# A short-sequence attention kernel: the whole output held on chip and stored in one run, four buffers for q and k, and an empty first trip of TensorE's loop

## The chip, the cores and the metric

The kernel runs on one core of a Trainium2 chip. A core has five engines that run their own instruction streams and meet only at semaphores: TensorE (PE; its weight loads are listed apart as PEld), VectorE (DVE), ScalarE (ACT), GpSimd (POOL) and SyncE (SP). Data move between the chip's main memory (HBM) and the on-chip memory (SBUF) by 16 DMA engines. Here GpSimd issues all loads and SyncE all stores. TensorE writes to PSUM, from which VectorE and ScalarE carry results to SBUF.

The metric is the device time of one execution in microseconds (us). The profile is one execution of its own, taken by the hardware profiler; its span runs from the first to the last instruction.

## The reference

For 32 x 12 heads, each with 128 rows of 64 elements, the kernel computes softmax attention:

```python
# q, k, v: (32, 12, 128, 64) float32
scale = 1.0 / np.sqrt(q.shape[-1])
scores = scale * np.matmul(q, k.transpose(0, 1, 3, 2))
attn = np.exp(scores - scores_max)
attn = attn / (np.sum(attn, axis=-1, keepdims=True) + 1e-8)
return np.matmul(attn, v).astype(np.float32)
```

Each of q, k, v and the output is 12.58 MB in float32. The loads cast to bf16 on the way, so 37.75 MB are read and 18.87 MB written into SBUF; the output is stored in float32.

## The kernel before

The work is cut into 48 units of 8 heads. Four units make a group (a "super" in the code). A group needs one load of q, one of k and one of v, 512 KB each as written in bf16, so there are 12 of each. The output goes out in 48 transfers of 256 KB.

A load brings many rows of a head into one partition, so that the runs in memory are long. TensorE then puts things in order: it transposes pairs of rows of q and k (through `pair`), and reorders v by matmuls with a selection matrix. A unit is then: scores (q times k), exp on ScalarE, values (times v, with a column of ones that gives the sum), and on VectorE the reciprocal and the product (`normalise`).

```python
NQ, NVB, NVE, NP, NT, NA, NO = 8, 2, 8, 4, 2, 4, 10      # buffers: q and k, v, ..., output
LATE, LOADED = 14, NU - 12                               # NU = 48

q_b = [sb(f"q_b{i}", [128, 2, 16 * D], bf16) for i in range(NQ)]
v_b = [sb(f"v_b{i}", [128, 4, RV * D], bf16) for i in range(NVB)]
o_sb = [sb(f"o_sb{i}", [128, 2 * 2 * RO * D], f32) for i in range(NO)]
# ... cut
```

The program is written in steps. In step u each engine gets, in this order: TensorE the transposes of a group ahead (T), the ordering of v of unit u+3 (V), the scores of u+1 (S) and the values of u (O); ScalarE copies the ordered v (K) and takes the exps of u+1; VectorE normalises u-1 (N), carries the transposes from PSUM (E) and makes the pairs for step u+2 (P), which is where it waits for loads.

```python
for u in steps:
    for t in t_at.get(u, []):        pe_transposes(t)
    for m in v_at.get(u, []):        pe_order_v(m); act_keep(m)      # m = u + 3
    if 0 <= u + 1 < NU:              pe_scores(u + 1); act_exps(u + 1)
    if 0 <= u < NU:                  pe_values(u)
    if 0 <= u - 1:                   dve_normalise(u - 1)
    for t in t_at.get(u, []):        dve_keep(t)
    for t in t_at.get(u + 2, []):    dve_pair(t)                     # waits for q or k, and for v
    # ... cut
```

GpSimd issues the loads in the order in which they are first needed: q0 k0 v0 q1 k1 v1 q2 k2 v2 q3 k3 v3 and so on. Each has a wait for its buffer:

```python
if kind == "v":
    if x >= NVB:                     # until v of the group two before is ordered
        deps = [("V", sum(vgroups[:x - NVB + 1]) - 1)]
    # ... cut
if x >= NQ:                          # q, k: until the pairs of the group NQ before are made
    deps = [("P", t) for t in t_order if t[0] == x - NQ and t[1] == j]
```

SyncE issues the stores. A store waits for its last unit plus `LATE` units, but not beyond unit 36, and the output buffers are used in turn, so `normalise` waits for the store ten before:

```python
last = first + n - 1
op("SP", ("store", c), emit, [("N", max(last, min(last + LATE, LOADED)))])

def dve_normalise(u):
    c, w, n, first = splace[u]
    dma = []
    if w == 0 and c >= NO:
        dma.append((s_o[c % NO], sum(16 * pieces(x) for x in range(c % NO, c, NO))))
    # ... cut
```

VectorE tells SyncE and GpSimd of its progress by marks on the pair copies (and, near the end, on `normalise` itself), so a store leaves after the first such mark behind the unit that it waits for.

TensorE's program is a loop of 7 trips, 8 steps to a trip. What does not exist in the first or in the last trip is skipped by a branch; a wait counts its semaphore down, so the same instructions serve each trip:

```python
nc.tensor.reg_mov(trip, 0)
with nc.tensor.Fori(0, TRIPS):
    for skipped, always, some in places:
        run_waits("PE", always)
        with nc.tensor.If_ne(trip, skipped):
            for o, w in some:
                run("PE", o, w)
    nc.tensor.reg_add(trip, trip, 1)
```

Of the kernel before, what the change touches and what calls it, by code (L numbers as in the profile page):

```python
# [10 lines left out]
def kernel(  # L11
# [7 lines left out]
    nc = tc.nc  # L19
    f32 = mybir.dt.float32  # L20
# [3 lines left out]
    B, H, S, D = q.shape  # L24
# [7 lines left out]
    NU = B * H // 8  # L32
    RO, SO = 4, S // 4
# [25 lines left out]
    stores = [1, 1] + [2] * ((NU - 4) // 2) + [1, 1]  # L59
# [5 lines left out]

    PERIOD = 8
    TRIPS = NU // PERIOD + 1


    t_at, v_at = {}, {}
    for s, (R, f) in enumerate(supers):
        J = R // 4
        for x in range(J):
            j, b = divmod(x, J // 2)
# [2 lines left out]
        v_at[m - 3] = [m]  # L79
    steps = range(min(t_at) - 2, NU + 1)  # L80

    NQ, NVB, NVE, NP, NT, NA, NO = 8, 2, 8, 4, 2, 4, 10

    LATE, LOADED = 14, NU - 12

    def sb(name, shape, dtype):
        return ctx.enter_context(nc.sbuf_tensor(name, shape, dtype))
# [11 lines left out]
    pair = [sb(f"pair{i}", [128, 8, 2, D], bf16) for i in range(NP)]  # L99
    qkT = [sb(f"qkT{i}", [128, 2, 16, S], bf16) for i in range(NT)]  # L100
    attnT = [sb(f"attnT{i}", [128, 2, 4, S], bf16) for i in range(NA)]
    o_sb = [sb(f"o_sb{i}", [128, 2 * 2 * RO * D], f32) for i in range(NO)]
    recip = [sb(f"recip{i}", [128, 2, RO], f32) for i in range(2)]
    qk_ps = ps("qk_ps", [128, 8 * S], bf16)
    s_ps = [ps(f"s_ps{i}", [128, 2, 4 * S], f32) for i in range(2)]
# [9 lines left out]
    sems = {name: tc.alloc_semaphore(name) for name in MARKS}  # L115
# [7 lines left out]
    def op(engine, key, emit, deps=(), marks=(), dma=()):  # L123
        o = Op()
        o.key, o.emit, o.deps, o.marks, o.dma = key, emit, deps, marks, dma
        assert key not in position, key
        position[key], engine_of[key] = len(program[engine]), engine
        program[engine].append(o)

    def counts():  # L130
        c = {}
        for name, e in MARKS.items():
            n, at = 0, []
            for o in program[e]:
                n += name in o.marks
                at.append(n)
            c[name] = at
        return c
# [120 lines left out]
    def normalise(u):  # L259
        c, w, n, first = splace[u]  # L260
        o4 = o_ps[:, :, :RO * (D + 1)].rearrange("p a (r e) -> p a r e", e=D + 1)
        r = recip[u % 2]
        nc.vector.reciprocal(r[:], o4[:, :, :, D]).then_inc(s_r, 1)  # L263
        nc.vector.wait_ge(s_r, u + 1)
        o = o_sb[c % NO][:, :n * 2 * RO * D].rearrange("p (a w e) -> p a w e", a=2, w=n)
        return nc.vector.tensor_mul(  # L266
            o[:, :, w, :].rearrange("p a (r d) -> p a r d", d=D),
            o4[:, :, :, :D],
            r[:].unsqueeze(3).to_broadcast([128, 2, RO, D]))
# [6 lines left out]
    s_q = [tc.alloc_semaphore(f"s_q{i}") for i in range(NQ)]  # L276
    s_k = [tc.alloc_semaphore(f"s_k{i}") for i in range(NQ)]
    s_v = [tc.alloc_semaphore(f"s_v{i}") for i in range(NVB)]
    s_o = [tc.alloc_semaphore(f"s_o{i}") for i in range(NO)]
    v_readers = {}  # L280
    for u in range(NU):
        for a in range(2):
# [58 lines left out]

    def dve_normalise(u):
        c, w, n, first = splace[u]
        dma = []
        if w == 0 and c >= NO:
            dma.append((s_o[c % NO], sum(16 * pieces(x) for x in range(c % NO, c, NO))))

        marks = ["dve_pe"] + (["dve_io"] if u + 8 > t_step[t_order[-1]] else [])
        op("DVE", ("N", u), lambda: normalise(u), [("O", u)], marks, dma)

    def pieces(c):

        first = sum(stores[:c])
        return 2 if 1 < stores[c] < supers[of_unit[first]][0] // 4 else 1

    def sp_store(c):
        n = stores[c]
        first = sum(stores[:c])
        R, f = supers[of_unit[first]]
        J = R // 4  # L360

        def emit():
            dst = o_rows[:, 2 * f:2 * f + 2 * J, :].rearrange("p (a w) e -> p a w e", a=2)[
                :, :, first - f:first - f + n, :]
            src = o_sb[c % NO][:, :n * 2 * RO * D].rearrange("p (a w e) -> p a w e", a=2, w=n)
            if pieces(c) == 1:
                nc.sync.dma_start(out=dst, in_=src).then_inc(s_o[c % NO], 16)
            else:
                for a in range(2):
                    nc.sync.dma_start(out=dst[:, a], in_=src[:, a]).then_inc(s_o[c % NO], 16)  # L370

        last = first + n - 1
        op("SP", ("store", c), emit, [("N", max(last, min(last + LATE, LOADED)))])

    def pool_load(kind, x):
        deps = []
# [50 lines left out]
    for c in range(len(stores)):  # L427
        sp_store(c)
# [10 lines left out]
    for _, kind, x in loads:  # L439
        pool_load(kind, x)  # L440

    c = counts()
# [4 lines left out]
    def waits_of(engine, o):  # L447
        out = []
        for name, value in needed(engine, o, c).items():
            have = seen[engine].get(name, 0)  # L450
            if value > have:
                out.append((name, value - have if engine == "PE" else value))
                seen[engine][name] = value
        return out

    def run_waits(engine, waits):
        for name, value in waits:
            i = ENGINE[engine].wait_ge(sems[name], value)  # L458
            if engine == "PE":
                i.then_inc(sems[name], -value)  # L460

    def run(engine, o, waits):
# [5 lines left out]
        for n, name in enumerate(o.marks):  # L468
            (i if n == 0 else e.drain()).then_inc(sems[name], 1)

    def tensor_program():

        ops, waits, when = {}, {}, {}
        for o in program["PE"]:
            place = at_step[o.key] % PERIOD, o.key[0]
            w = waits_of("PE", o)
            assert waits.setdefault(place, w) == w and not o.dma, (o.key, w, waits[place])
            when.setdefault(place, []).append((at_step[o.key] // PERIOD + 1, o.emit is None))
            if at_step[o.key] // PERIOD == 2:
                ops[place] = o  # L480
        places = []
        for place in [(l, kind) for l in range(PERIOD) for kind in "TVSO"]:
            trips = [t for t, empty in when[place] if not empty]
            assert trips in (list(range(TRIPS - 1)), list(range(1, TRIPS))), (place, trips)
            waiting = len(when[place]) > len(trips)
            assert not waiting or len(when[place]) == TRIPS
            skipped = 0 if trips[0] else TRIPS - 1
            if waiting or not places or places[-1][0] != skipped:
                places.append((skipped, waits[place] if waiting else [], []))
            places[-1][2].append((ops[place], [] if waiting else waits[place]))  # L490
        trip = ctx.enter_context(nc.tensor.register("trip"))
        nc.tensor.reg_mov(trip, 0)
        with nc.tensor.Fori(0, TRIPS):
            for skipped, always, some in places:
                run_waits("PE", always)
                with nc.tensor.If_ne(trip, skipped):
                    for o, w in some:
                        run("PE", o, w)
            nc.tensor.reg_add(trip, trip, 1)

    with nc.Block() as block:
        @block.gpsimd
        def _(_e):
            for i, o in enumerate(program["POOL"]):
                if i == 2:
                    nc.gpsimd.wait_ge(s_zero, 1)
                    nc.gpsimd.affine_select(  # L507
                        out=ident[:], in_=ident[:], compare_op=mybir.AluOpType.not_equal,
                        fill=1.0, base=0, pattern=[[-1, 128]], channel_multiplier=1,
                    ).then_inc(s_id, 1)  # L510
                run("POOL", o, waits_of("POOL", o))

        @block.tensor
        def _(_e):
            tensor_program()

        @block.scalar
        def _(_e):
            for o in program["ACT"]:
                run("ACT", o, waits_of("ACT", o))  # L520

        @block.vector
        def _(_e):
            for t in sel.values():
                nc.vector.memset(t[:], 0.0)  # L525
            nc.vector.memset(ident[:], 0.0).then_inc(s_zero, 1)
            for t in v_e:
                nc.vector.memset(t[:, :, D:D + 1], 1.0)
            nc.vector.wait_ge(s_id, 1)

            for jv in range(2):
                nc.vector.tensor_copy(  # L532
                    sel[16][:].rearrange("p h v (x y s) -> p h v x y s", x=2, y=2)[:, :, jv, :, jv, :],
                    ident[:].rearrange("p (h s x) -> p h x s", h=8, x=2))
            for o in program["DVE"]:
                run("DVE", o, waits_of("DVE", o))

        @block.sync
        def _(_e):
            for o in program["SP"]:  # L540
                run("SP", o, waits_of("SP", o))
            for i in range(NO):
                nc.sync.wait_ge(s_o[i], sum(16 * pieces(x) for x in range(i, len(stores), NO)))


# [28 lines left out]
```

The softmax here doesn't subtract the row's maximum and nothing guards it: scores larger than these inputs give would overflow.

## Time and profile before

| | before |
|---|---|
| time, median of 3 runs (us) | 142.29 (142.08 to 142.77) |
| span of the profiled execution (us) | 141.3 |
| busy: PE, DVE, ACT, POOL (us) | 97.5, 89.8, 74.2, 26.8 |
| mean granted TensorE clock | 0.923 |
| read from HBM, written to it (MB) | 37.75, 12.58 |
| issues of the stores, first to last (us) | 57.1 to 136.9 |
| issues of v's loads, first to last (us) | 3.3 to 110.7 |

How to read the profile: the page cuts the span into 40 slices, and each digit is a busy share in tenths; under it stand the GB/s that the DMA engines moved (as written). A window line gives, for a stretch A:B, its length, the busy time and count of instructions of each engine, the granted clock, the share of the 16 DMA engines that was busy (it can exceed 1, as packets overlap), and GB/s. A wait line reads: who waited, at which line of the kernel, for whom, then the total in us, how often, and the longest. A timeline line reads: start, length, engine, line, operation, tiles, count, and in brackets the idle time before it and what ended it; "issue" is time in which the engine waited for nothing that the profile shows. The records hold each DMA packet as well, with its queue, size and time.

### The profile page before, as it was taken

To read this page: it belongs to the slowest core of one execution; us is meant where nothing else is said; L and a number is where in the kernel's file an instruction comes from. 1 tells how busy PE (TensorE), PEld (TensorE's weight loads), DVE (VectorE), ACT (ScalarE), POOL (GpSimd) and SP (SyncE) were. 2 spreads that over 40 slices of the span, in tenths; PEclk is the share of its full clock that TensorE was granted. 3 is DMA by queue.
4 is the path that set the end of the run, shared out by engine and by line. 5 is a ranking of instruction groups with operands and counts; after the bars stand their busy time and mean duration, and the time that the engine had idled before them with its cause. 6 is when DMAs were issued, how large, how long until landed. Compare 5 with 4: busy or idle time off the path is not lost. (4 is left out here: it accounts for less than half of the span.)

```text
span 141.3 us, 6998 instructions
## 1 busy us (share of the span) xinstructions
PE 97.5 (69%) x3072; PEld 68.9 (49%) x3072; DVE 89.8 (64%) x204; ACT 74.2 (52%) x97; POOL 26.8 (19%) x41
## 2 busy tenths in 40 slices
PE   0051939999959789796695698595594798597510
PEld 0041625766646566574463465373363466465310
DVE  2143632989779696974963964964974767685540
ACT  3000206877847758576375177284484447559800
POOL 6910000506060240601402401400600200000000
PEclk9999996999999999999999689999999559999855
DMA  2999999699999999999999999999999999999982
GB/s 14 186 206 211 202 206 179 81 210 188 181 200 143 212 189 187 219 176 235 246 236 240 253 236 240 252 235 242 253 235 241 255 206 313 379 382 369 335 281 77
DMA packets 25928, 31.55 MB, mean 223 GB/s; under 512 B 1345, under 2 KB 19777, under 8 KB 25921
## 3 DMA queue, kind: packets, MB, share of 16 engines
q0 software_dynamic: 12864, 18.88, 76.5%
q1 hardware_dynamic: 13056, 12.59, 28.0%
q8 instruction: 4, 0.07, 0.2%
q14 instruction: 4, 0.02, 0.0%
HBM read 37.75 MB, written 12.58 MB: 356 GB/s over the span
## 5 line engine op out<-in xcount | busy, mean ns | idle before, releaser
L231 ACT CAST v_e<-v_ps 128x512 bf16<-128x512 f32 x48 | 28.2, 588 | 58.4 <-PE v_ps L185 58.4
L236 ACT ACTIVATE attnT<-s_ps 128x1024 bf16<-128x1024 f32 x48 | 49.4, 1029 | 0.3 <-PE s_ps L211 0.2
L171 PE MATMUL qk_ps<-ident,pair 128*128 128x128 bf16 x384 | 32.5, 233 | 16.5 <-PEq L458 15.7
L254 DVE COPY qkT<-qk_ps 128x1024 bf16<-128x1024 bf16 x48 | 32.8, 683 | 6.1 <-PE qk_ps L171 5.0
L185 PE MATMUL v_ps<-v_b,sel 128*32 128x256 bf16 x768 | 33.0, 295 | 3.1 <-issue 2.1
L171 PEld LDWEIGHTS qk_ps<-ident,pair 128*128 128x128 bf16 x384 | 24.3, 104 | 21.5 <-issue 20.6
L266 DVE TENSOR_TENSOR o_sb<-o_ps,recip 128x512 f32<-128x512 f32 x48 | 33.2, 691 | 1.7
L223 PE MATMUL o_ps<-v_e,attnT 128*32 128x65 bf16 x1536 | 21.7, 200 | 18.2 <-PEq L458 18.1
L223 PEld LDWEIGHTS o_ps<-v_e,attnT 128*32 128x32 bf16 x1536 | 16.1, 100 | 24.2 <-issue 21.2
L381 POOL DMA_DIRECT2D v_b<-in_v_dram x12 | 9.2, 770 | 83.4 <-PE v_ps L185 83.4
L245 DVE COPY pair<-k_b 128x1024 bf16<-128x1024 bf16 x24 | 11.0, 460 | 20.2 <-DMA v_b<-in_v_dram 20.2
L185 PEld LDWEIGHTS v_ps<-v_b,sel 128*32 128x32 bf16 x768 | 17.2, 100 | 9.6 <-issue 4.5
L211 PE MATMUL s_ps<-qkT 64*128 64x128 bf16 x384 | 19.9, 226 | 0.6 <-PEq L458 0.5
L263 DVE RECIPROCAL recip<-o_ps 128x8 f32<-128x8 f32 x48 | 9.7, 202 | 12.9 <-PE o_ps L223 6.6
L211 PEld LDWEIGHTS s_ps<-qkT 64*128 64x128 bf16 x384 | 11.3, 97 | 11.5 <-issue 11.5
L245 DVE COPY pair<-q_b 128x1024 bf16<-128x1024 bf16 x24 | 10.1, 422 | 3.4 <-DMA q_b<-in_q_dram 3.2
L393 POOL DMA_DIRECT2D q_b<-in_q_dram x12 | 8.7, 727 | 1.0 <-SPq L92 1.0
L393 POOL DMA_DIRECT2D k_b<-in_k_dram x12 | 8.8, 734 | 0.0
L231 ACT ACT_TABLE_LOAD x1 | 1.3, 1283 | 1.0 <-SPq L92 1.0
L532 DVE COPY sel<-ident 128x128 bf16<-128x128 bf16 x2 | 0.4, 225 | 1.7 <-POOL ident L507 1.7
L525 DVE MEMSET sel<- 128x256 uint32 x1 | 0.3, 272 | 1.1 <-SPq L92 1.1
L507 POOL TENSOR_SCALAR_AFFINE_SELECT ident<-ident 128x128 bf16<-128x128 bf16 x1 | 0.3, 312 | 0.1
(6 smaller groups left out, 0.8 us busy)
## 6 DMA issues: line engine op xcount, KB each, us to landing
out_dram<-o_sb SPq DMA_DIRECT2D x48, 256.0 KB, 7.0
q_b<-in_q_dram POOLq DMA_DIRECT2D x12, 512.0 KB, 11.4
k_b<-in_k_dram POOLq DMA_DIRECT2D x12, 512.0 KB, 13.5
v_b<-in_v_dram POOLq DMA_DIRECT2D x12, 512.0 KB, 9.8
```

The lines of the kernel that those rows point to most:

```text
L171: i = nc.tensor.transpose(p[:, :, r4, jj, :], x[:, r].rearrange("p a d -> p (a d)"), ident[:])
L185: x = nc.tensor.matmul(t[r4 * 32:(r4 + 1) * 32, i, :, :], lhsT=pick[:, w * nh + i, jv, :], rhs=v_b[g % NVB][:, :n, (4 * jv + r4) * D:(4 * ...
L211: i = nc.tensor.matmul(t[:, a, h, :], lhsT=x[p, 1, 4 * w + h, :], rhs=x[p, 0, 4 * w + h, :], start=True, stop=True)
L223: y = nc.tensor.matmul(t[h * SO:(h + 1) * SO, a, r * (D + 1):(r + 1) * (D + 1)], lhsT=x[:, a, h, r * SO:(r + 1) * SO], rhs=v_e[m % NVE][:, ...
L231: return nc.scalar.copy(v_e[m % NVE][:, :, :D], v_ps[:].rearrange("p (n e) -> p n e", e=D))
L236: return nc.scalar.activation(out=attnT[u % NA][:].rearrange("p a h (r s j) -> p (a h r) s j", r=4, j=J), in_=s_ps[u % 2][:].rearrange("p ...
L245: return nc.vector.tensor_copy(pair[t_index[t] % NP][:], src[:, 8 * b:8 * b + 8])
L254: return nc.vector.tensor_copy(x.rearrange("p h (r j s) -> p (h r) j s", r=4, j=J)[:, :, 2 * b:2 * b + 2, :].rearrange("p x j s -> p x (j ...
L263: nc.vector.reciprocal(r[:], o4[:, :, :, D]).then_inc(s_r, 1)
L266: return nc.vector.tensor_mul(o[:, :, w, :].rearrange("p a (r d) -> p a r d", d=D), o4[:, :, :, :D], r[:].unsqueeze(3).to_broadcast([128, ...
L381: op("POOL", ("load", kind, x), lambda: nc.gpsimd.dma_start(out=v_b[x % NVB][:, :n, :], in_=v_rows[:, first:first + n, :],).then_inc(s_v[x ...
L393: nc.gpsimd.dma_start(out=bufs[x % NQ][:], in_=rows[R][:, n:n + 2, :]).then_inc(sm[x % NQ], 16)
```

## The change

Three things change. First, each output transfer has a buffer of its own (96 KB for each partition in all), `normalise` no longer waits for stores, and no store is issued before unit 34 is normalised; the stores then follow one another as units are done. The aim is to part the loads from the stores. Second, q and k get four buffers each instead of eight, which frees the room. Third, TensorE's loop gets one more trip, ahead of the others, in which every block is skipped; ScalarE and VectorE raise the semaphores by what the waits of that trip count down. It is meant to bring the loop's instructions onto the chip while the first loads are under way.

```diff
-    NQ, NVB, NVE, NP, NT, NA, NO = 8, 2, 8, 4, 2, 4, 10
-    LATE, LOADED = 14, NU - 12
+    NQ, NVB, NVE, NP, NT, NA = 4, 2, 8, 4, 2, 4
+    HELD = NU - 14
-    o_sb = [sb(f"o_sb{i}", [128, 2 * 2 * RO * D], f32) for i in range(NO)]
+    o_sb = [sb(f"o_sb{c}", [128, n * 2 * RO * D], f32) for c, n in enumerate(stores)]
@@ dve_normalise
-        dma = []
-        if w == 0 and c >= NO:
-            dma.append((s_o[c % NO], sum(16 * pieces(x) for x in range(c % NO, c, NO))))
@@ sp_store
-        op("SP", ("store", c), emit, [("N", max(last, min(last + LATE, LOADED)))])
+        op("SP", ("store", c), emit, [("N", max(last, HELD))])
@@ tensor_program
+        for skipped, always, some in places:
+            for name, value in always:
+                extra[name] = extra.get(name, 0) + value
-        nc.tensor.reg_mov(trip, 0)
-        with nc.tensor.Fori(0, TRIPS):
+        for r, x in ((trip, 0), (step, 2), (a, 0), (b, 0)):
+            nc.tensor.reg_mov(r, x)
+        with nc.tensor.Fori(0, TRIPS + 1):
             for skipped, always, some in places:
                 run_waits("PE", always)
-                with nc.tensor.If_ne(trip, skipped):
+                with nc.tensor.If_ne(b if skipped else a, 0):
                     for o, w in some:
                         run("PE", o, w)
-            nc.tensor.reg_add(trip, trip, 1)
+            nc.tensor.reg_add(trip, trip, step)
+            nc.tensor.reg_mov(step, 1)
+            nc.tensor.reg_add(a, trip, 1)
+            nc.tensor.reg_alu(a, a, 2, mybir.AluOpType.logical_shift_right)
+            nc.tensor.reg_alu(b, trip, 7, mybir.AluOpType.bitwise_and)
@@ scalar and vector, ahead of their programs
+            nc.scalar.drain().then_inc(sems["act_pe"], extra["act_pe"])
+            nc.vector.drain().then_inc(sems["dve_pe"], extra["dve_pe"])
@@ cut: the stores' semaphores, ten before, are four now
```

More of the change, by code (lines that the diff above doesn't have):

```diff
@@ L264, in normalise @@
         nc.vector.wait_ge(s_r, u + 1)
-        o = o_sb[c % NO][:, :n * 2 * RO * D].rearrange("p (a w e) -> p a w e", a=2, w=n)
+        o = o_sb[c][:].rearrange("p (a w e) -> p a w e", a=2, w=n)
         return nc.vector.tensor_mul(
@@ L278 @@
     s_v = [tc.alloc_semaphore(f"s_v{i}") for i in range(NVB)]
-    s_o = [tc.alloc_semaphore(f"s_o{i}") for i in range(NO)]
+    s_o = [tc.alloc_semaphore(f"s_o{i}") for i in range(4)]
     v_readers = {}
@@ L343, in dve_normalise @@
         c, w, n, first = splace[u]
-        dma = []
-        if w == 0 and c >= NO:
-            dma.append((s_o[c % NO], sum(16 * pieces(x) for x in range(c % NO, c, NO))))
         marks = ["dve_pe"] + (["dve_io"] if u + 8 > t_step[t_order[-1]] else [])
-        op("DVE", ("N", u), lambda: normalise(u), [("O", u)], marks, dma)
+        op("DVE", ("N", u), lambda: normalise(u), [("O", u)], marks)
     def pieces(c):
@@ L364, in emit @@
                 :, :, first - f:first - f + n, :]
-            src = o_sb[c % NO][:, :n * 2 * RO * D].rearrange("p (a w e) -> p a w e", a=2, w=n)
+            src = o_sb[c][:].rearrange("p (a w e) -> p a w e", a=2, w=n)
             if pieces(c) == 1:
-                nc.sync.dma_start(out=dst, in_=src).then_inc(s_o[c % NO], 16)
+                nc.sync.dma_start(out=dst, in_=src).then_inc(s_o[c % 4], 16)
             else:
                 for a in range(2):
-                    nc.sync.dma_start(out=dst[:, a], in_=src[:, a]).then_inc(s_o[c % NO], 16)
+                    nc.sync.dma_start(out=dst[:, a], in_=src[:, a]).then_inc(s_o[c % 4], 16)
         last = first + n - 1
-        op("SP", ("store", c), emit, [("N", max(last, min(last + LATE, LOADED)))])
+        op("SP", ("store", c), emit, [("N", max(last, HELD))])
     def pool_load(kind, x):
@@ L469, in run @@
             (i if n == 0 else e.drain()).then_inc(sems[name], 1)
+    extra = {}
     def tensor_program():
@@ L490, in tensor_program @@
             places[-1][2].append((ops[place], [] if waiting else waits[place]))
-        trip = ctx.enter_context(nc.tensor.register("trip"))
-        nc.tensor.reg_mov(trip, 0)
-        with nc.tensor.Fori(0, TRIPS):
+        for skipped, always, some in places:
+            for name, value in always:
+                extra[name] = extra.get(name, 0) + value
+        trip, step, a, b = (ctx.enter_context(nc.tensor.register(x)) for x in ("trip", "step", "a", "b"))
+        assert TRIPS == 7
+        for r, x in ((trip, 0), (step, 2), (a, 0), (b, 0)):
+            nc.tensor.reg_mov(r, x)
+        with nc.tensor.Fori(0, TRIPS + 1):
             for skipped, always, some in places:
                 run_waits("PE", always)
-                with nc.tensor.If_ne(trip, skipped):
+                with nc.tensor.If_ne(b if skipped else a, 0):
                     for o, w in some:
                         run("PE", o, w)
-            nc.tensor.reg_add(trip, trip, 1)
+            nc.tensor.reg_add(trip, trip, step)
[3 more added lines that the diff above has]
+            nc.tensor.reg_alu(b, trip, 7, mybir.AluOpType.bitwise_and)
     with nc.Block() as block:
@@ L541, in _ @@
                 run("SP", o, waits_of("SP", o))
-            for i in range(NO):
-                nc.sync.wait_ge(s_o[i], sum(16 * pieces(x) for x in range(i, len(stores), NO)))
+            for i in range(4):
+                nc.sync.wait_ge(s_o[i], sum(16 * pieces(x) for x in range(i, len(stores), 4)))
 _INS = ['q', 'k', 'v']
```

## The prediction

> **What bounds the kernel now.** I first read the slices of the page and the DMA queues, then the windows cut where the traffic changes, then the waits, and last the order of work in the first 30 us. The chain that ended last is of little use: it goes back only 1.7 us, from the last unit's output to its matmuls.
>
> The page's slices (40 of 3.53 us) and its queue list:
>
> ```profile
> DMA  2999999699999999999999999999999999999982
> GB/s 14 186 206 211 202 206 179 81 210 188 181 200 143 212 189 187 219 176 235 246 236 240 253 236 240 252 235 242 253 235 241 255 206 313 379 382 369 335 281 77
> q0 software_dynamic: 12864, 18.88, 76.5%
> q1 hardware_dynamic: 13056, 12.59, 28.0%
> q8 instruction: 4, 0.07, 0.2%
> ```
>
> The DMA engines are busy almost throughout, while PE is busy for 69% and DVE for 64% of the span. The bound is the traffic: 18.88 MB of loads (counted as written, in bf16; twice that is read) on q0 and 12.59 MB of stores on q1. The windows give the rates (last columns: granted clock, DMA share, GB/s):
>
> ```profile
> 3.00:6.00 3.00, 0.00 (x0) 0.00 (x0) 0.36 (x2) 0.00 (x0) 2.92 (x6) 1.00 1.02 156
> 6.00:24.00 18.00, 10.18 (x120) 6.65 (x120) 7.01 (x14) 2.73 (x4) 1.67 (x3) 0.91 1.15 207
> 24.00:27.00 3.00, 3.00 (x116) 2.31 (x112) 2.26 (x7) 2.58 (x4) 2.15 (x3) 1.00 0.35 39
> 27.00:42.00 15.00, 12.77 (x449) 9.20 (x447) 12.58 (x28) 11.03 (x15) 4.36 (x6) 1.00 1.12 194
> 42.00:45.00 3.00, 3.00 (x107) 2.10 (x108) 2.94 (x6) 1.83 (x3) 0.02 (x1) 1.00 0.86 133
> 45.00:57.00 12.00, 10.52 (x376) 7.62 (x371) 9.40 (x23) 8.75 (x12) 2.15 (x3) 1.00 1.13 194
> 66.00:111.00 45.00, 32.21 (x1040) 22.58 (x1032) 30.06 (x67) 24.76 (x34) 9.09 (x13) 0.94 1.14 242
> 117.00:129.00 12.00, 9.34 (x356) 6.75 (x352) 8.69 (x18) 8.03 (x11) 0.00 (x0) 1.00 1.10 364
> 129.00:138.00 9.00, 4.04 (x192) 2.78 (x176) 4.50 (x10) 4.57 (x6) 0.00 (x0) 0.73 0.93 317
> 138.00:141.30 3.30, 0.00 (x0) 0.00 (x0) 0.00 (x0) 0.00 (x0) 0.00 (x0) 0.50 0.20 67
> ```
>
> Loads alone run at 194 to 207 GB/s, stores alone at 380 (the slices 379 and 382), both together at 242. Two holes stand out while there are loads left to do: 24 to 27 us (39 GB/s) and 42 to 45 us (133). The waits, the timeline of TensorE and that of GpSimd say where the first comes from:
>
> ```profile
> POOL v_b L381 <- PE v_ps L185: 83.4, 10, 16.7
> DVE recip L263 <- DMA out_dram<-o_sb: 6.3, 6, 2.1
> ```
>
> ```profile
> 18.15 0.27 PE L185 MATMUL v_ps<-v_b,sel 128*32 128x256 bf16 x1 [0.22 <-PEq L458]
> 20.57 1.04 PE L185 MATMUL v_ps<-v_b,sel 128*32 128x256 bf16 x15 [2.15 <-issue]
> ```
>
> ```profile
> 24.41 0.74 POOL L381 DMA_DIRECT2D v_b<-in_v_dram  x1 [16.75 <-PE v_ps L185]
> ```
>
> GpSimd issues all loads in one order; v has two buffers, so group 2 of v (and all of q and k behind it) waits until TensorE has ordered v of unit 3. That came at 24.1 us, because TensorE stood still for 2.15 us inside a block of 16 matmuls, on nothing but "issue". The eight loads issued before were all landed by 25 us, so the queue ran dry.
>
> [...] in 66 to 111 us I count 147 GB/s of loads and 95 of stores in the packet records; 147/197 + 95/380 = 0.75 + 0.25 = 1.00. Mixing costs nothing and gains nothing. [...] 207 GB/s written is 414 read. [...] q8 has just four packets of 16 KB in the whole run, at 2.3, 12.0, 18.1 and 24.0 us, [...] the third fetch lies in the 2.15 us hole. [...] Here v's group 2, issued at 24.41 us into an empty queue, landed at 30.0: 5.6 us, of which its data need 3.0.
>
> **The change part by part.**
> 1. The floor of the traffic. Rows of q and k run at 210 GB/s (30.5 to 33.5 us), rows of v, half as long, at about 176 (fitted over the load-only stretches): 12.58/0.2105 + 6.29/0.176 = 59.8 + 35.7 = 95.5 us, or 7.96 us for a group of four units (197 GB/s on average). Stores: 12.58/0.380 = 33.1. Together 128.6 us. The change moves the same bytes in the same rows, so this stays.
> 2. What the 141.3 us hold beside it: 12.7 us. Start 3.0 + 0.5; hole at 24 us 2.4; hole at 42 us 0.9; small holes of the load-only stretches and at the first stores 1.2; the mixed stretch 0.5; from 129 us on, where the last stores wait for the last units, 4.2, of which 2.3 lie between the last packet (139.0) and the end.
> 3. The empty trip. TensorE waits for its first transposes until 7.7 us anyway. Eight registers' moves, its skipped branches and four fetches (0.9 us each as packets, on an almost idle queue) fit before that or shortly after; what k's first pair releases, at 12.75 us, is the first thing that matters. It takes out the 2.15 us and about 0.5 us before 13.5 us (the fetch at 12.0). The third unit's matmuls then stand at the pace of transpose and copy (1.92 us a step): v of unit 3 is ordered at about 21 instead of 24.1 us, v's group 2 is issued near 21.3. Its data started 2 to 3.3 us after the issue, so at about 24.5; the queue empties at 24.3 (mean engine) to 25.0 (last). The hole of 2.4 shrinks to about 0.3: gain 2.1. The two added drains and increments cost nothing on the path.
> 4. The stores in one run. They are issued after the pair copy behind unit 34's output. That copy (k of group 10) also waits for v of group 10. From then on there are 35 units to store and nothing keeps q1 from being full: the last units are done around 121 us (v of group 11 landed near 105, plus the 16.1 us from there to the last unit's output now), when q1 still has 12 us of backlog. So the tail of 4.2 becomes the bare 2.3: gain 1.9. The mixed stretch's 0.5 goes as well.
> 5. What it takes away. Until now stores filled holes of the load queue: 0.5 us lost in 51 us. The 39 us from 27 to 66, nearly all loads, lost 2.1 us beside the first hole. Now the load-only stretch lasts from 24 to about 95 us. The loop of v (v of group g lands; 9.5 us later unit 4g+3 is ordered; v of g+2 is issued and lands 7.4 to 8.1 us after) closes in (9.5 + 7.4)/2 = 8.45 us a group, against 7.96 for the traffic; measured landings of v 3, 4 and 5 were 8.6 and 8.4 apart. With the first hole gone the queue has more in hand; I take 8.2 a group over nine groups, 2.2 us lost. In before 2.1 of such losses stood (0.9 + 1.2), so this costs 0.1.
> 6. q and k in four buffers rather than eight: v's wait keeps q and k at most three groups ahead, so no load waits for them. Zero.
>
> Sum: 128.6 + 3.5 + 0.3 + 2.2 + 0.3 (handover to the stores) + 2.3 = 137.2 us of span. The median time lies 1.0 above the profiled span (142.29 against 141.3): 138.2; since two of the losses may be smaller I put it at 137.9 us, 3.1% faster.
>
> **The rivals.**
> A. Holding the stores back uncovers the loop of v. If it closes in 8.5 to 8.7 us, unit 34 comes 2.5 to 4.5 us later, and the stores with it: 140 to 142 us, no gain. For it: 8.4 to 8.6 measured. Against it: those groups came just after the first hole, with an empty queue.
> B. Mixed reads and writes cost more than I see, so that parting them gains more: 133 to 135. Against it: the sum of 1.00 above.
> C. The empty trip fetches nothing useful, or runs past 12.7 us: the first hole stays, 140.3. [...]
> D. The units after 34 become the end, if the stores' backlog starves v of group 11. Stores with a backlog left loads about 70% of the engines at 111 to 117 us, so v of group 11 is 3 us late at most, against 12 us of slack: nothing.
>
> **Range and chances.** The floor with no hole left is 128.6 + 3.5 + 2.3 = 134.4 of span, 135.4 of time; A at its worse end is 141. I give 135.3 to 140.2. Two per cent faster means below 139.44: A or C alone would miss it, so 0.78; within 2% 0.20; slower 0.02.
>
> **What would show it.** Step 3: no "issue" wait of 2 us on the v matmuls, GpSimd's issue of v group 2 near 21 us, all four 16 KB packets before 11 us, 24 to 27 us near 190 GB/s. Step 4: no store before about 95 us, then 380 GB/s to the end with DMA share above 1; the last matmul near 120 us. Step 5: the distance of v's issues, 8.0 to 8.4 us, and the mean rate of 27 to 90 us (195 expected). Step 6: no q or k load with a wait of its own. I am wrong if loads alone stay at or below 190 GB/s (A), if the first hole stays (C), or if stores alone over 30 us do not hold 380.

## The result and the profile after

| | before | changed |
|---|---|---|
| time, median of 4 runs each (us) | 142.53 | 151.63 (151.49 to 151.97) |
| span of the profiled execution (us) | 141.3 | 149.4 |
| first transposes of TensorE (us) | 7.7 | 18.8 |
| issue of v's group 2 (us) | 24.4 | 30.4 |
| first store issued (us) | 57.1 | 106.6 |

The changed kernel is slower: ratio 1.065, 95% interval 1.061 to 1.069. (Executions slowed by a disturbance are left out of the ratios, so these need not equal the quotient of two medians.) I had forecast 137.9 us.

The slices of the changed kernel's page, 3.73 us each:

```profile
DMA  2999994049999999999999999999999999999993
GB/s 15 200 204 216 203 213 89 0 54 208 185 173 196 157 212 179 195 179 203 193 179 203 151 206 165 186 168 175 203 205 357 379 380 367 358 350 343 344 344 111
```

The hole after 24 us, which the empty trip was to close, is three times as long; one slice moves nothing at all. Loads then go on alone to 110 us, at 151 to 212 GB/s. The stores follow in one run, as planned, but the slices 380, 367, 358, 350, 343, 344 show a rate that falls.

Its windows (columns as before: busy time of each engine, granted clock, DMA share, GB/s):

```profile
6.00:24.00 18.00, 3.47 (x36) 2.70 (x40) 3.28 (x7) 0.00 (x0) 1.67 (x3) 1.00 1.14 207
24.00:33.00 9.00, 9.00 (x204) 5.98 (x196) 5.79 (x14) 5.25 (x8) 2.14 (x3) 1.00 0.12 14
33.00:105.00 72.00, 62.82 (x2191) 45.43 (x2192) 60.83 (x134) 51.80 (x69) 17.41 (x24) 1.00 1.09 185
111.00:123.00 12.00, 10.31 (x385) 7.40 (x384) 9.68 (x21) 8.88 (x13) 0.00 (x0) 1.00 1.10 363
123.00:147.00 24.00, 3.27 (x163) 2.19 (x152) 4.04 (x9) 3.83 (x5) 0.00 (x0) 0.60 1.03 348
```

Up to 24 us the traffic is what it was (207 GB/s), but TensorE was busy for 3.5 us in that stretch, where it had been busy for 10.2. From 24 to 33 us the DMA engines do next to nothing (share 0.12) while TensorE catches up. From 33 to 105 us there are only loads, at 185 GB/s; before, the loads alone from 27 to 57 us had 188, their hole at 42 us included. At the end, stores alone run at 348.

What held TensorE, from the timelines of TensorE and of GpSimd in the changed kernel (start, length, engine, line, operation, and in brackets the idle time before; PEq and PEldq are the names under which the trace lists TensorE's waits and branches):

```profile
18.78 1.03 PE L172 MATMUL qk_ps<-ident,pair 128*128 128x128 bf16 x8 [18.78 <-PEq L456]
```

```profile
30.37 0.75 POOL L379 DMA_DIRECT2D v_b<-in_v_dram  x1 [22.70 <-PE v_ps L186]
```

The first transposes come 11.1 us later than before, and v's group 2, whose issue waits for v of unit 3, 6.0 us later. The source view of the branch that skips a block (duration in ns: least, median, greatest) names the cause. In three short stretches of the empty trip it shows one branch each:

```profile
L502 PEldq COMPARE_BRANCH  x1: 2698/2698/2698, 2.4 to 2.4; - x1
L502 PEldq COMPARE_BRANCH  x1: 5017/5017/5017, 6.1 to 6.1; - x1
L502 PEldq COMPARE_BRANCH  x1: 5070/5070/5070, 12.0 to 12.0; - x1
```

Of the trip's twelve skipping branches eight took 0.21 to 0.22 us and the first 0.35. These three took 2.7, 5.0 and 5.1 us: 12.8 of the 16 us between 2 and 18 us. In the packet records the 16 KB packets of the instruction queue q8 start at 2.6, 8.8, 14.7 and 20.3 us; the first three lie inside those three branches, and the fourth lies behind the trip, where the branches beside it took 0.21 and 0.07 us.

The packet records also split the span as the prediction's sum did (bytes of a stretch over 210.5, 176 and 380 GB/s give its work, the rest of the stretch is lost). The stretches end at 24, 33, 105, 123 and 147 us, without the empty trip at 24, 28, 100, 121 and 142 us. The last column is the first experiment below.

| us of span | predicted | changed | changed, without the empty trip |
|---|---|---|---|
| traffic at full rates | 128.6 | 128.6 | 128.6 |
| start | 3.5 | 3.3 | 3.4 |
| hole from 24 us on | 0.3 | 8.3 | 2.9 |
| gaps in the stretch of loads alone | 2.2 | 4.5 | 5.3 |
| handover from loads to stores | 0.3 | 0.3 | 0.3 |
| stores alone below 380 GB/s | 0 | 2.0 | 1.6 |
| end: last packets (0.4 to 0.5 us, measured columns) and what follows (2.0) | 2.3 | 2.3 | 2.4 |
| sum, of unrounded rows | 137.2 | 149.4 | 144.5 |

### The profile page after: what moved, and what is told of

The parts are those of the page before. It is cut to its first block, busy times and chain, and to the rows that moved or that the text cites. A ratio compares the mean times of both kernels' runs of the same rounds, so it can differ in the third digit from the quotient of the medians.

```text
span 149.4 us, 7032 instructions
## 1 busy us (share of the span) xinstructions
PE 92.4 (62%) x3072; PEld 66.1 (44%) x3072; DVE 89.4 (60%) x204; ACT 74.0 (50%) x97; POOL 26.6 (18%) x41
## 5 line engine op out<-in xcount | busy, mean ns | idle before, releaser
L172 PE MATMUL qk_ps<-ident,pair 128*128 128x128 bf16 x384 | 31.4, 228 | 26.9 <-PEq L456 25.9
L172 PEld LDWEIGHTS qk_ps<-ident,pair 128*128 128x128 bf16 x384 | 23.5, 102 | 31.6 <-issue 30.4
L186 PE MATMUL v_ps<-v_b,sel 128*32 128x256 bf16 x768 | 31.1, 284 | 0.7 <-PEq L456 0.7
L224 PE MATMUL o_ps<-v_e,attnT 128*32 128x65 bf16 x1536 | 20.9, 197 | 8.5 <-PEq L456 8.4
L224 PEld LDWEIGHTS o_ps<-v_e,attnT 128*32 128x32 bf16 x1536 | 15.2, 97 | 13.8 <-issue 9.7
L212 PE MATMUL s_ps<-qkT 64*128 64x128 bf16 x384 | 19.2, 220 | 0.6 <-PEq L456 0.5
L186 PEld LDWEIGHTS v_ps<-v_b,sel 128*32 128x32 bf16 x768 | 16.5, 98 | 6.5 <-issue 1.5
L246 DVE COPY pair<-k_b 128x1024 bf16<-128x1024 bf16 x24 | 11.0, 457 | 11.1 <-DMA v_b<-in_v_dram 11.0
```

What stands on the lines that cost most here:

```text
L172: i = nc.tensor.transpose(p[:, :, r4, jj, :], x[:, r].rearrange("p a d -> p (a d)"), ident[:])
L186: x = nc.tensor.matmul(t[r4 * 32:(r4 + 1) * 32, i, :, :], lhsT=pick[:, w * nh + i, jv, :], rhs=v_b[g % NVB][:, :n, (4 * jv + r4) * D:(4 * ...
L212: i = nc.tensor.matmul(t[:, a, h, :], lhsT=x[p, 1, 4 * w + h, :], rhs=x[p, 0, 4 * w + h, :], start=True, stop=True)
L224: y = nc.tensor.matmul(t[h * SO:(h + 1) * SO, a, r * (D + 1):(r + 1) * (D + 1)], lhsT=x[:, a, h, r * SO:(r + 1) * SO], rhs=v_e[m % NVE][:, ...
L246: return nc.vector.tensor_copy(pair[t_index[t] % NP][:], src[:, 8 * b:8 * b + 8])
```

## The experiments

My theory after the result: the long branches are waits for the packets of q8, which come late while the DMA engines are full of loads (share 1.14 from 6 to 24 us); TensorE has to sit them out before it may do anything, and this starves the loads (8 us); holding the stores uncovers the gaps of the v loop (2.3 us more than I took) and makes a run of stores that does not hold its rate (2 us). Rivals: the held stores are the whole loss; the four buffers are at fault; all skipping branches are slow, with or without a packet.

**1. The empty trip taken out.** Seven trips again; the two drains, which raised the semaphores for the empty trip, are gone:

```diff
-        for r, x in ((trip, 0), (step, 2), (a, 0), (b, 0)):
+        for r, x in ((trip, 2), (step, 1), (a, 0), (b, 2)):
-        with nc.tensor.Fori(0, TRIPS + 1):
+        with nc.tensor.Fori(0, TRIPS):
```

> The changed kernel without its empty trip (7 trips, no added increments); stores still held, q and k still in four buffers. If the empty trip is what starved the loads, the first transposes come back to 7.7 us, v's group 2 is issued near 24.4 us instead of 30.4, and everything behind it moves by 6 us: 151.6 - 6 = 145.6 us, which is still 2% above the kernel before, so that holding the stores costs about 3 us by itself. Rival 1, holding the stores is the whole loss: no change, 150 to 152. Rival 2, holding the stores gains what I predicted and only the trip is at fault: 138 to 140.

Measured: 148.45 us where the kernel before had 143.16 beside it; ratio 1.038 (1.029 to 1.047). The first transposes are back at 7.8 us and v's group 2 is issued at 25.0. So the trip is a large part and not the whole; both plain rivals fall. I had expected 145.6 us; the hole shrinks by 5.4 us rather than 6, and the gaps grow by 0.8. The windows of this kernel:

```profile
24.00:28.00 4.00, 4.00 (x144) 2.83 (x136) 3.32 (x8) 3.00 (x4) 2.15 (x3) 0.94 0.34 56
28.00:100.00 72.00, 63.31 (x2171) 45.59 (x2160) 60.07 (x134) 50.91 (x69) 17.41 (x24) 0.98 1.10 183
109.00:121.00 12.00, 8.62 (x316) 6.07 (x312) 7.93 (x18) 8.42 (x11) 0.00 (x0) 1.00 1.09 378
121.00:142.00 21.00, 1.99 (x108) 1.40 (x104) 2.89 (x7) 2.05 (x2) 0.00 (x0) 0.56 1.04 351
```

The old hole is there again (56 GB/s from 24 to 28 us). Loads alone run at 183 GB/s for 72 us, although neither TensorE (63 of 72 us busy) nor VectorE (60) is full, and the stores fall from 378 to 351 GB/s.

**2. The empty trip alone, put into the kernel before.** The new loop and the two drains, nothing else.

> The kernel before with the empty trip alone (stores and buffers as before). If the trip delays TensorE as in the changed kernel, its first transposes start near 18.8 us, v's group 2 is issued near 30.4 us and the hole in the load traffic grows from 2.4 to about 8.4 us: 142.5 + 5.5 to 6 = 148 us. If the loss needs the held stores (rival 1), the time stays at 142.5.

Measured: 149.64 against 143.16, ratio 1.043 (1.034 to 1.052). First transposes at 19.5 us, v's group 2 at 31.0. The longest branch of the trip takes 6.20 us, and the window shows the same hole as in the changed kernel:

```profile
L504 PEldq COMPARE_BRANCH  x12: 207/212/6197, 1.6 to 17.8; - x12
24.00:33.00 9.00, 8.75 (x199) 5.68 (x200) 5.59 (x12) 4.63 (x7) 1.96 (x3) 1.00 0.09 16
```

The trip needs nothing else to cost 6.5 us. Alone the two parts cost 4.3 and 3.8%, together 6.5: they do not quite add, and why is open.

**3. Two empty trips.**

```diff
-        for r, x in ((trip, 0), (step, 2), (a, 0), (b, 0)):
+        for r, x in ((trip, 0), (step, 0), (nxt, 2), (a, 0), (b, 0)):
-        with nc.tensor.Fori(0, TRIPS + 1):
+        with nc.tensor.Fori(0, TRIPS + 2):
-            nc.tensor.reg_mov(step, 1)
+            nc.tensor.reg_add(step, nxt, 0)
+            nc.tensor.reg_mov(nxt, 1)
```

(and twice the increments of the two semaphores).

> The changed kernel with a second empty trip behind the first. If the first trip's 16 us are fetches of instruction blocks, which are done once, the second has only its branches and register steps: 15 branches of 0.27 us and 0.6 us of the rest, about 4.5 us; first transposes near 23.3 us, time near 156 us, no further branch longer than 0.4 us. Rival, the skipping branches or the waits themselves are slow: another 16 us, first transposes near 35 us, time near 167.

Measured, one execution: 154.9 us; first transposes at 22.3 us. The source view of the same branch, over the first empty trip and over the second with the start of the first real one:

```profile
L503 PEldq COMPARE_BRANCH  x12: 207/212/4650, 1.6 to 16.3; - x12
L503 PEldq COMPARE_BRANCH  x14: 68/207/213, 17.4 to 22.1; - x14
```

In the first trip the longest branch is 4.65 us, in the second 0.21. The second trip lasts 4.3 us, from 17.1 to 21.4. The same branches are not slow there; what was slow happened in the first trip alone.

**4. The loads held back until the empty trip is over.**

```diff
+            nc.tensor.drain().then_inc(s_trip, 1)       # end of each trip
+            nc.gpsimd.wait_ge(s_trip, 1)                # ahead of the first load
```

> The changed kernel, but GpSimd issues its first load only when TensorE has ended the empty trip (a semaphore raised at the end of each trip). It tells why the second and third fetch took 5.0 us and the first 2.7. If they had to get through DMA queues full of loads, all three take about 2.7 us now and the trip ends near 13 us. If a fetch at those places takes 5 us whatever else runs, the trip still ends near 18 us. The total is worse in either case, as the loads start so much later: about 155 to 160 us.

Measured, one execution: 155.97 us; the first load is issued at 13.1 us. The same three branches, now with nothing else on the DMA engines:

```profile
L502 PEldq COMPARE_BRANCH  x1: 2558/2558/2558, 2.4 to 2.4; - x1
L502 PEldq COMPARE_BRANCH  x1: 2497/2497/2497, 6.0 to 6.0; - x1
L502 PEldq COMPARE_BRANCH  x1: 2670/2670/2670, 9.3 to 9.3; - x1
```

So with no load under way each of the three took 2.5 to 2.7 us, and with loads under way the longest took 4.6 to 6.2 us (5.07 in the changed kernel, 6.20 and 4.65 in experiments 2 and 3). The loads are what stretches the second and the third; the first starts at 2.4 us, before the first load moves (3.0). Since each of the three holds one 16 KB packet of q8, I call them fetches; that is my reading of the times. The packet records show where the time goes: with idle engines (experiment 4) the 16 KB packet starts 0.1 to 0.3 us after the branch, behind loads 2.3 to 3.9 us after it (second and third fetch of the changed kernel and of experiments 2 and 3); the packet then takes 0.9 to 1.0 us, and the branch ends 1.3 to 1.5 us after it in either case. What grows is the wait ahead of the packet. With the trip over before the loads the hole is gone (200 GB/s from 15 to 33 us and 208 from 33 to 42), so the purpose of the empty trip was sound; but it costs 11.6 us of later loads.

**5. Stores from unit 14 on instead of 34**, in the kernel of experiment 1: `HELD = 14`.

> The changed kernel without its empty trip, and with stores from unit 14 on instead of 34 (one number: HELD = 14; q and k still in four buffers, every store in a buffer of its own). If parting loads from stores is what cost the rest, because the gaps that the v loop leaves in the load queue (5.3 us from 28 to 100 us) go unfilled, the stores fill them again and the time comes back to that of the kernel before, 142 to 144 us. If the four buffers of q and k are to blame instead, it stays at 147 to 148.

Measured: 144.31 against 142.70, ratio 1.007 (1.002 to 1.012). One number takes the ratio from 1.038 to 1.007: what remained after experiment 1 is nearly all the holding back of the stores.

**6. Every second store from GpSimd**, in the kernel of experiment 1 (GpSimd issues its stores behind all its loads):

```diff
+        queue = (nc.sync, nc.gpsimd)[c % 2]
-        op("SP", ("store", c), emit, [("N", max(last, HELD))])
+        op(("SP", "POOL")[c % 2], ("store", c), emit, [("N", max(last, HELD))])
```

> The changed kernel without its empty trip; every second store is issued by GpSimd, which is idle once the loads are out, instead of SyncE. In the stretch of stores alone the rate fell from 380 to 343 GB/s, where SyncE issued one transfer of 256 KB every 0.76 us. If SyncE's issue sets that pace, two issuers bring 375 to 380 GB/s to the end and 1.5 to 2 us: 145.5 us. If the DMA engines or the memory give no more, the rate stays at 343 and the time at 147 to 148.

Measured: 147.15 against 142.70, ratio 1.025 (1.017 to 1.033). The window of stores alone is no better for the second issuer:

```profile
121.00:142.00 21.00, 1.97 (x112) 1.34 (x108) 3.02 (x7) 2.15 (x3) 2.14 (x3) 0.60 1.00 332
```

332 GB/s, against 351 in experiment 1 in the same window: my expectation failed. It does not clear SyncE either, because the stores that GpSimd issued went out in other packets (6.29 MB in packets of 4 KB, where SyncE's have 1 KB, by the packet records).

**7. The wait for v one step later**, in the kernel of experiment 1. VectorE waited for v's load at the pair copy, two steps before TensorE orders it; now at the copy from PSUM one step before:

```diff
@@ dve_pair
-        for m in v_at.get(t_step[t], []):
-            g, w, n, first = vplace[m]
-            if w == 0:
-                dma.append((s_v[g % NVB], 16 * (g // NVB + 1)))
@@ dve_keep
+        for m in v_at.get(t_step[t] + 1, []):
+            g, w, n, first = vplace[m]
+            if w == 0:
+                dma.append((s_v[g % NVB], 16 * (g // NVB + 1)))
@@ pe_order_v: the dependence moves with it
-        deps = [("K", m - 1)] + ([("P", t_at[vstep_of[m]][0])] if w == 0 else [])
+        deps = [("K", m - 1)] + ([("E", t_at[vstep_of[m] - 1][0])] if w == 0 else [])
```

> The changed kernel without its empty trip, with VectorE's wait for a load of v moved one step later (from the pair copy two steps before its use to the copy from PSUM one step before it). It shortens the loop from v's landing to the issue of v two groups on from 9.5 to about 7.7 us. If that loop paces the stretch of loads alone (8.46 us a group against 7.96 for the traffic), v's issues come 8.0 to 8.1 us apart, the 5.3 us lost between 28 and 100 us fall to 1 to 2, and the time is 143.5 to 144.5. If loads alone just run at 8.4 us a group, nothing changes: 147 to 148.

Measured: 143.63 against 142.70 (medians; no interval, the runs spread too much), where experiment 6, which differs from experiment 1 only in who issues the stores, had 147.15 beside it. The issues of v lie (97.19 - 25.23) / 9 = 8.00 us apart, against (101.10 - 25.00) / 9 = 8.46 in experiment 1. The window of loads alone:

```profile
28.00:96.00 68.00, 62.41 (x2210) 45.35 (x2195) 61.77 (x138) 51.85 (x70) 17.61 (x24) 1.00 1.13 193
```

193 GB/s instead of 183, with the same loads in the same order. So the loop through VectorE's wait paced the loads, not the traffic.

**8. The kernel before, with loads that never starve.** The later wait, and two more loads ahead of the first that must wait:

```diff
-        loads.append((vstep_of[m] - 1.5, "v", g))
+        loads.append((vstep_of[m] + (2.5 if g > 1 else -1.5), "v", g))
```

> The kernel before (interleaved stores, no empty trip) with the later v wait and with the loads of q and k of group 3 issued ahead of v of group 2 (v of group g behind q and k of group g+1 from there on), so that two more loads are under way while TensorE fetches its loop. It should close the hole at 24 us (2.4 us) without any empty trip and most of the small ones: 138 to 139.5 us, faster than the kernel before. If the later landing of v holds up the units instead, 142 to 144.

Measured: 139.36 against 142.70, ratio 0.973 (0.965 to 0.981): faster than both kernels. Its windows:

```profile
24.00:28.00 4.00, 4.00 (x128) 2.95 (x122) 2.73 (x6) 2.91 (x4) 2.14 (x3) 1.00 1.12 210
28.00:57.00 29.00, 26.58 (x948) 19.28 (x941) 26.36 (x59) 22.11 (x30) 7.25 (x10) 1.00 1.16 208
126.00:136.90 10.90, 3.00 (x160) 2.03 (x152) 3.96 (x9) 3.74 (x5) 0.00 (x0) 0.75 0.68 231
```

The hole is closed (210 GB/s from 24 to 28 us) though v's group 2 is still issued at 24.1 us: the queue holds two more loads by then. That is the work of these loads: with the later wait alone (experiment 7) the hole stays, at 27 GB/s from 24 to 28 us. How much of the whole gain belongs to each of the two was not measured. What remains is the end, where the last stores wait for the last units (share 0.68).

**9 and 10. The same two changes with held stores**, from unit 34 and from unit 22 on, without the empty trip.

> The held stores (unit 34) without the empty trip, with the later v wait and with q and k of group 3 ahead of v of group 2, as in the run before that beat the kernel before with interleaved stores. It asks whether holding is worth anything once the loads never starve. By the sum of the traffic: start 3.5, loads 95.5, stores 33.1 plus 1.8 for the slower second half of a long run of stores, end 2.9: 137 to 138 us of span, 138 to 139.5 us of time, level with the interleaved version (139.4). If holding still costs 3 us or more: 142 and up.

> The same with stores from unit 22 on. If a long run of stores alone is slower only after some 12 us, an earlier start that lets the stores share the engines with the loads for longer shortens that run and saves 1 to 2 us: 137 to 138.5 us. If the loads that then share with the stores delay the last units more than that, 140 to 142.

Measured: 140.62 and 138.89 against 143.28; ratios 0.980 (0.971 to 0.989) and 0.969 (0.959 to 0.978). Both lie a little above what I had expected (138 to 139.5 and 137 to 138.5). Once the loads are fed, holding to unit 34 is no longer a loss against the kernel before. Stores from unit 22 on gave the fastest version of the study, but its interval overlaps that of experiment 8, so whether holding gains anything is not shown.

**11. Stores alone.** VectorE fills the output buffers with ones (there are 26 for the 48 transfers; 22 of them hold two transfers each), SyncE issues all stores; loads and the attention are left out.

> Only the 48 stores: VectorE fills the 48 output buffers with ones, then SyncE issues all stores one after the other; loads and all the attention are left out. If the fall from 380 to 343 GB/s comes of a long run of stores as such, it shows here about 12 us after the first, and the last stores come 0.76 us apart. If it needs what stands around it in the full kernel (an issuer that waits for units, loads just before), 380 GB/s hold to the end, 0.69 us apart, 33.1 us in all.

Measured in one execution. Windows of the first and the last stretch (here VectorE and GpSimd are the only engines, then clock, DMA share, GB/s):

```profile
30.00:34.00 4.00, 0.00 (x0) 0.00 (x0) 1.00 1.03 341
61.00:64.00 3.00, 0.00 (x0) 0.00 (x0) 1.00 1.02 343
```

Neither expectation holds: the rate is 340 to 343 GB/s from the start, with the stores 0.77 us apart from the sixth on. The 380 GB/s of the kernel before belong to a stretch in which the stores had piled up behind the loads: from 119 to 127 us six or seven were issued and not yet landed. In the changed kernel there were eight of these at 114 us, and three or four from 134 us on, when SyncE issued one every 0.77 us; in experiment 11 there are three or four throughout. So no fatigue of a long run shows: the stores landed 0.69 us apart while a backlog drained (121 to 127 us in the kernel before, 114 to 124 us in the changed one), and 0.76 to 0.77 us apart without one (from 134 us on in the changed kernel, and in experiment 11). The pace fits SyncE's issue (0.73 us each, 0.04 between, DMA share 1.03 instead of 1.09), but experiment 6 did not confirm it; what sets 0.77 is open.

**12. Four buffers for q and k in the kernel before**, nothing else.

> The kernel before with q and k in four buffers each instead of eight, nothing else. I said zero, because v's wait keeps q and k at most three groups ahead: 142 to 143.5 us, within 0.5% of the kernel before. If buffers did matter, q's and k's issues would show waits of their own for the pair copies, and the time would be 144 or more.

Measured: 143.09 against 143.28, ratio 1.000 (0.996 to 1.004).

## Why the prediction was wrong

- *What bounds the kernel, and the floor.* Right, as far as the runs go: both kernels move the same bytes, 128.6 us at full rates, and where the engines were fed the loss was near zero (0.3 us from 3 to 24 us, none from 111 to 123). That the table's sum closes shows nothing, since what is not work is counted as lost.
- *Step 3, the empty trip: the step that failed.* I wrote that the skipped branches and "four fetches (0.9 us each as packets, on an almost idle queue) fit before that or shortly after". I took the time of a packet for the time of a fetch. What TensorE lost was the whole of the long branch: 2.5 to 2.7 us with idle DMA engines (experiment 4), 4.6 to 6.2 for the longest ones behind loads (the changed kernel, experiments 2 and 3). And the engines are not idle: the loads are under way from 3 us on, which is the very time that the trip was to use. Even with idle engines the trip lasted to 13.0 us (experiment 4), well past the 7.7 us of the first transposes. I expected v's group 2 at 21.3 us; it came at 30.4, and the hole went from 2.4 to 8.3 us instead of to 0.3. The records of the kernel before held a warning: in its stall of 2.15 us TensorE went on only 1.6 us after the end of the third q8 packet (19.0 us), so the wait outlasted the packet. How long TensorE waited for the other packets there is not shown, as most of such a time would lie beside waits for loads. What the step foresaw for the time after the trip held: the stall of 2.15 us inside the v matmuls is gone, and from 24 to 33 us TensorE is busy for 9.00 of 9.00 us.
- *Step 4, stores in one run.* The mechanism was right (first store only after the pair copy behind unit 34, though at 106.6 us and not near 95; DMA share above 1 to the last packet, 0.3 us of handover, 2.3 us of end). The rate was mis-sized: 380 GB/s were read off a stretch with a backlog. It cost 2.0 us, which is all that the shorter tail was to bring.
- *Step 5, the gaps in the stretch of loads alone.* The loop of v was named, with 8.45 us a group, and then softened to 8.2 for a queue with "more in hand". Measured: (105.62 - 30.37) / 9 = 8.36 in the changed kernel, 8.46 without the trip, and 4.5 and 5.3 us lost where I took 2.2. Experiment 7 shows the loop by shortening it (8.00).
- *Step 6, four buffers.* Right: 1.000.
- *The rivals.* A, the loop uncovered by the held stores, was right in kind, and still too mild: without the trip the held stores made the kernel 3.8% slower, against 0.7% with early ones (experiments 1 and 5). C saw that the trip might run past 12.7 us and the first hole stay, but not that the hole could grow. B fell: parted, neither loads nor stores ran above the rates of the floor, and experiment 5, which mixes them for longer, was faster than experiment 1. (The mixed stretch of the prediction splits into 148 and 93 GB/s rather than 147 and 95; its sum stays 1.00.) D held: the last matmuls end at 129 us, 18 us ahead of the last packet.
- *The range* ended at 140.2, below the 141 that I gave for rival A at its worse end, and it held no cost for the empty trip: the trip was put as a gain that might not come.

## What to carry to other kernels

A branch that held a 16 KB instruction packet cost 2.5 to 2.7 us here with no load under way and up to 6.2 us behind loads. Before running a loop empty, compare such a sum with the time that the engine has to spare: here the first transposes came at 7.7 us without the trip, and the trip ended at 13.0 us with idle DMA engines (experiment 4) and at 18.0 us behind loads (the changed kernel). Where loads are paced by a loop of buffer, wait and issue, transfers in the other direction that fill the gaps are worth keeping until the loop is fixed: here moving one wait by one step and letting two loads go ahead gained 2.7%, where the held stores alone lost 3.8% and the whole change 6.5%. And a rate read off a backlog was not the rate of the same transfers without one (380 against 342 GB/s).

## What the runs showed of the hardware that I had not expected

- The branches that held one of q8's 16 KB packets took 2.5 to 2.7 us with no load under way (experiment 4), and the longest 4.6 to 6.2 us behind loads (the changed kernel, experiments 2 and 3), though the packets themselves took 0.9 to 1.1 us in the kernel before and in the changed one. Each of these two had four such packets, 64 KB, in all its trips. The last started at 24.0 and 20.3 us, after the branch that ends the first trip (21.1 and 18.0 us), and none came later.
- In these two kernels 28 of the 36 branches that skip their block took 0.20 to 0.22 us and five took 0.32 to 0.35; the other three are the long ones. A branch that falls through took 0.06 to 0.08 us.
- Stores of 256 KB in packets of 1 KB, issued by SyncE, came 0.77 us apart (342 GB/s) without a backlog (experiment 11), and 0.69 us apart (380 GB/s) while one drained (the kernel before).
